# Storing results one pass later: a softmax-times-V kernel on one core

## The chip, the cores and the metric

The kernel runs on one core of a Trainium2 chip. A core has five engines that run side by side and signal each other with semaphores: TensorE (matmuls and transposes; PE in the profile, its weight loads PEld), VectorE (DVE), ScalarE (ACT), GpSimd (POOL) and SyncE (SP), which here does nothing but issue DMA transfers. The transfers themselves are carried out by 16 DMA engines. The metric is device time in microseconds (us), the median of several executions.

## The reference

```python
def reference(scores, v):               # scores 8 x 12 x 1024 x 1024, v 8 x 12 x 1024 x 64, float32
    scores_max = np.max(scores, axis=-1, keepdims=True)
    attn = np.exp(scores - scores_max)
    attn = attn / (np.sum(attn, axis=-1, keepdims=True) + 1e-8)
    return np.matmul(attn, v).astype(np.float32)
```

Batch and heads together are 96 independent heads (BH). The scores are 402.65 MB, V and the result 25.17 MB each, so a kernel that touches everything once moves 453 MB.

## The kernel before, in words

**Tiling.** Two heads are worked on together (T = 2): each has 64 of the 128 partitions, and each partition holds 16 consecutive rows of its head (R = 16). A "row" r below is therefore a tile of 128 partitions x 1024 scores, 512 KB in HBM. Two heads make a block of 16 rows (8 MB), two blocks (K = 2, k = 0 and 1) make a pass of four heads (AHEAD = 4), and the loop `with tc.For_i(0, BH, AHEAD)` runs 24 passes, n0 = 0, 4, ... 92.

**What happens to a row.** ScalarE takes the exponential and writes it as fp16 (L384; two rows per instruction, or one row where `late` holds). It subtracts no maximum. TensorE transposes the row in eight pieces into PSUM (L397), VectorE copies the transposed piece to SBUF (L409 for two rows, L405 for one row where `late` holds), and TensorE multiplies it in eight matmuls with V (L152, in `finish`). The V operand `vones` has a column of ones behind each head's 64 columns, so the product also holds the sum of the row. `finish` of a row comes LAG = 3 rows after its transposes. After every third row, and after row 15, VectorE takes the reciprocal of the sums (L132) and writes the quotient into `out_bufs[k]` (L140, `normalise`).

**Buffers.** There is one score buffer `s_bufs[k]` per block, 64 KB per partition, one result buffer `out_bufs[k]` per block, eight exp buffers of two rows (`p_bufs`), two of each for the transposed rows in PSUM and SBUF. A load into `s_bufs[k]` for the next pass can thus only be issued when ScalarE has read the last row of that block in this pass. `out_bufs[k]` may be written again only when its store has landed.

**V.** A DMA brings V of four heads into `v_sb` one pass ahead (`load_v`). GpSimd rearranges it into `vones[k]` with eight small casts (L255, `spread_v`): for k = 0 after row 15 of block 0, for k = 1 at the end of the pass.

**A guard.** Since no maximum is subtracted, the kernel watches its sums. ScalarE adds up the absolute values of `v_sb` (L266, `watch_v`), VectorE folds these and the reciprocals into a minimum and a maximum (`fold`, L284 and L285), and at the end `judge` counts the partitions in which all is in range. If any is not, a general routine is run instead; with this data it is not.

**The order of transfers.** SP issues all DMAs, in the order in which the code has them, and they go through one queue. In a pass the order is: next scores of block 0 (`load_first`, in the code at row 6 of block 1), store of block 0, next scores of block 1, store of block 1, V of two passes ahead (`last`). In all but the last passes a load is one DMA of 8 MB. In the passes n0 = 84 and 88 it is cut in pieces, (4, 6, 6) rows for block 0 and (4, 4, 4), then the store, then (2, 1, 1) for block 1. In pass 92 loads are skipped by a condition, and `end` stores block 1 in two parts, 12 rows and 4. The DMAs in the body take eight semaphores in turn, and a DMA waits until the one that last used its semaphore has landed.

**Order on the engines.** The order of TensorE's work is written out by `in_line`. The ifs on n0 are branches that each engine takes on its own; `branch_at` ties the branch of `load_first`, and that of `watch_v` (row 13 of block 1), to a place in TensorE's order.

Of the kernel before, what the change touches and what calls it, by code (L numbers as in the profile page):

```python
# [8 lines left out]
FP32 = mybir.dt.float32  # L9
FP16 = mybir.dt.float16  # L10
# [16 lines left out]
def kernel(  # L27
# [6 lines left out]
    nc = tc.nc  # L34
    P = 128
# [4 lines left out]
    BH = B * H  # L40
    assert SQ % P == 0 and SK % P == 0
    C = SK // P
    EB = 2
# [35 lines left out]
    def buffers(pool, count, shape, dtype, name):  # L79
        return [pool.tile(shape, dtype, name=f"{name}{k}") for k in range(count)]  # L80

    s_bufs = buffers(sb_pool, K, [P, R, SK], FP32, "s_nat")
    v_sb = sb_pool.tile([P, C // L, S, L, D], FP32, name="v_sb")
    p_bufs = buffers(sb_pool, 8, [P, EB, SK], FP16, "p_nat")
    pt_bufs = buffers(sb_pool, 2, [P, EB, SK], FP16, "pt")
    out_bufs = buffers(sb_pool, K, [P, R, D], FP32, "out_sb")
    small_pool = ctx.enter_context(tc.tile_pool(name="small", bufs=1))
    seen = small_pool.tile([P, 1 + K * R + 2], FP32, name="seen")
    nc.gpsimd.memset(seen, 1.0)
# [1 line left out]


    psO_bufs = buffers(ps_pool, 4, [P, 512], FP32, "psO")
    turn = {}

    def take(bufs):
# [8 lines left out]
    def after(a, b):  # L105

        tc.add_manual_dep(
            a.ins,
            b.ins.name,
            mybir.DependencyInfo(mybir.DependencyClass.NoSync, mybir.DependencyReason.DATA),  # L110
            reason="order",
        )
# [49 lines left out]
        if r == R - 1 and k < K - 1:  # L162
            spread_v(k)

    def store(n0, k):

        to = out_rows.rearrange("(m x) y -> m x y", x=P)[bass.ds((n0 + T * k) // T, 1)]
        to = to.rearrange("o x y -> (o x) y")
        send(nc.sync.dma_start(out=to, in_=out_bufs[k][:].rearrange("x r d -> x (r d)")))

    def send(dma):
        for other in stores:
            apart(dma, other)
            apart(other, dma)
        apart(dma, dma)
        stores.append(dma)
        queue(dma)

    def end():

        cut = (GROUPS - 2) * G
        for a, b in ((0, cut), (cut, R)):
            send(
                nc.sync.dma_start(
                    out=out_rows[(BH - T) * W : BH * W, a * D : b * D],
                    in_=out_bufs[K - 1][:, a:b].rearrange("x r d -> x (r d)"),
                )
            )

# [30 lines left out]
            )  # L220
            r += rows

    def branch_at(op):

        after(op, line[-1])

    def load_first(n0):

        before = queued[-1:]
        n = (n0 + AHEAD) % BH  # L230
        with tc.If(n0 < BH - 3 * AHEAD) as cmp:
            load(0, n)
            branch_at(queued[-1])
        with cmp.Else():
            queued[:] = before
            load(0, n, (4, 6, 6), cond=(n0 < BH - AHEAD))
            branch_at(queued[-1])
        line.append(queued[-1])

    def load_v(n, **cond):  # L240

# [20 lines left out]
    def watch_v():  # L262


        junk = p_bufs[0][:].rearrange("p r k -> p (r k)")
        return nc.scalar.activation(  # L266
            out=junk,
            in_=v_sb[:].rearrange("p h s l d -> p (h s l d)"),
            func=mybir.ActivationFunctionType.Abs,
            scale=1.0 / SUM_MAX,  # L270
            accum_out=seen[:, K * R + 1 : K * R + 2],
        )
# [78 lines left out]
    def last(n0, bank):  # L351

        before = queued[-1:]
        k = K - 1
        with tc.If(n0 < BH - AHEAD) as cmp:
            spread_v(k)
            n = (n0 + AHEAD + T * k) % BH
            with tc.If(n0 < BH - 3 * AHEAD) as cmp2:
                queued[:] = before
                load(k, n)  # L360
                store(n0, k)
                load_v((n0 + 2 * AHEAD) % BH)
            with cmp2.Else():
                queued[:] = before
                load(k, n, (4, 4, 4))
                store(n0, k)
                load(k, n, (2, 1, 1), 12)
                load_v(BH - AHEAD, cond=(n0 < BH - 2 * AHEAD))
        with cmp.Else():
            queued[:] = before  # L370
            end()
            judge(bank)

    def heads(n0):

        for k in range(K):
            st = dict(psO=[take(psO_bufs) for g in range(GROUPS)])
            for r in range(R):
                late = k == K - 1 and r >= R // 2
                if r % EB == 0:  # L380
                    p_nat, psT2, pt2 = take(p_bufs), take(psT_bufs), take(pt_bufs)
                    rows = 1 if late else EB
                    for g in range(0, EB, rows):
                        exp = nc.scalar.activation(  # L384
                            out=p_nat[:, g : g + rows, :].rearrange(
                                "p r (x v) -> p x r v", v=Q * L
                            ),
                            in_=s_bufs[k][:, r + g : r + g + rows, :].rearrange(
                                "p r (i x l) -> p x (r i) l", i=Q, l=L
                            ),  # L390
                            func=EXP,
                        )
                        rewrite(p_nat, exp)
                p_row = p_nat[:, r % EB, :].rearrange("p (h q l) -> p h l q", q=P, l=L)
                psT, pt = psT2[:, r % EB, :], pt2[:, r % EB, :]
                for c in range(C):
                    turned = nc.tensor.transpose(  # L397
                        out=psT[:, c * P : (c + 1) * P],
                        in_=p_row[:, c // L, c % L, :],
                        identity=ident16[:],  # L400
                    )
                    in_line(turned)
                    other_bank(psT2, r % EB, turned)
                if late:
                    copy = nc.vector.tensor_copy(out=pt, in_=psT)  # L405
                    rewrite(pt2, copy)
                    other_bank(psT2, r % EB, copy)
                elif r % EB == EB - 1:
                    copy = nc.vector.tensor_copy(out=pt2[:], in_=psT2[:])  # L409
                    rewrite(pt2, copy)  # L410
                if r == 6 and k == K - 1:
                    load_first(n0)
                    store(n0, 0)
                if r == 13 and k == K - 1:
                    with tc.If(n0 < BH - AHEAD):
                        watch = watch_v()
                        branch_at(watch)
                    line.append(watch)
                pending.append((n0, k, r, pt, st))
                while len(pending) > (LAG - 1 if late and r >= R - EB else LAG):  # L420
                    finish(pending.pop(0))
        while pending:
            finish(pending.pop(0))
        fold()
        last(n0, st["psO"][-1])
# [52 lines left out]
```

## Time and profile before

| what | value |
|---|---|
| runs | 1065.61, 1065.82, 1065.95 us; median 1065.82 |
| the profiled execution | 1065.58 us; its span, first to last instruction, 1063.8 us |
| DMA queue | 453 MB in 19584 packets, busy 99.1% of 16 engines' span, 426 GB/s on average |
| TensorE / weight loads | 77% / 74% of the span busy |
| ScalarE | 71%; 278.5 us of waiting for scores |
| VectorE / GpSimd | 66% / 22% |
| granted TensorE clock | 0.875 of full speed on average |
| one pass in the middle | about 43.6 us (load at 453.63, the same load of the next pass at 497.19) |

The page gives, for each engine, the time in which it was executing; a second part cuts the span in 40 slices and gives the busy share in tenths. A line such as "L384 ACT ..." is a group of instructions of one source line: busy time, mean duration in ns, then the idle time of the engine just before them and what ended it. In a timeline, a line is start, duration, engine, source line, operation, tiles, and in brackets the idle time ahead with its releaser. "Issue" lines of SP give the moment at which a DMA was put into the queue, not when it ran.

### The profile page before, as it was taken

How to read it: one execution, taken by the hardware profiler on the slowest of the kernel's cores; microseconds unless marked ns; L12 is line 12 of the kernel's file. 1: busy time of each engine (PE TensorE's matmuls, PEld its weight loads, DVE VectorE, ACT ScalarE, POOL GpSimd, SP SyncE). 2: the span in 40 equal slices, each digit the busy share in tenths (PEclk: the TensorE clock that was granted, in tenths of full speed). 3: DMA queues.
4: the chain of work that ended last, by engine and by line, in shares of the span. 5: the costliest groups of instructions: out<-in, count | busy, mean ns of one | idle time of the engine just before them, and what ended most of it. 6: DMA issues, size and time to landing. Idle time of an engine off the chain costs nothing. (4 is left out here: it accounts for less than half of the span.)

```text
span 1063.8 us, 33293 instructions
## 1 busy us (share of the span) xinstructions
PE 814.6 (77%) x12289; PEld 790.1 (74%) x12289; DVE 706.8 (66%) x1395; ACT 754.3 (71%) x530; POOL 239.0 (22%) x400
## 2 busy tenths in 40 slices
PE   2588778886877768886788778886788868887967
PEld 2488767786877768886777778876787867777967
DVE  1467766776667757676577765776667756677858
ACT  4477577776777667766777577775777667768965
POOL 3031130211312113112031130311312113112131
PEclk9788988888898978899888887998888898988989
DMA  9999999999999999999999999999999999999995
GB/s 394 435 429 431 414 434 453 414 453 430 418 453 414 432 455 414 453 414 432 452 416 451 407 443 451 416 448 427 426 448 419 423 437 441 414 453 413 430 415 228
DMA packets 19587, 453.04 MB, mean 426 GB/s; under 512 B 2176, under 2 KB 2304, under 8 KB 8960
## 3 DMA queue, kind: packets, MB, share of 16 engines
q1 hardware_dynamic: 19584, 452.99, 99.1%
q8 instruction: 3, 0.05, 0.0%
HBM read 437.26 MB, written 25.17 MB: 435 GB/s over the span
## 5 line engine op out<-in xcount | busy, mean ns | idle before, releaser
L384 ACT ACTIVATE p_nat<-s_nat 128x2048 f16<-128x2048 f32 (+1 forms) x480 | 707.1, 1557 | 292.5 <-DMA s_nat<-in_scores_dram 278.5
L397 PE MATMUL psT<-ident,p_nat 128*128 128x128 f16 x6144 | 525.5, 238 | 215.5 <-ACT p_nat L384 213.4
L397 PEld LDWEIGHTS <-p_nat 128*128 128x128 f16 x6144 | 442.3, 120 | 227.4 <-ACT p_nat L384 226.2
L409 DVE COPY pt<-psT 128x2048 f16<-128x2048 f16 x288 | 352.4, 1224 | 319.0 <-PE L152 159.0
L152 PE MATMUL psO<-vones,pt 128*128 128x130 f16 x6144 | 504.6, 229 | 28.4 <-DVE pt L405 17.7
L152 PEld LDWEIGHTS <-pt 128*128 128x128 f16 x6144 | 408.0, 102 | 40.7 <-DVE pt L405 21.9
L255 POOL CAST vones<-v_sb 32x512 f16<-32x512 f32 x392 | 238.1, 607 | 811.6 <-PE psT L397 360.9
L140 DVE TENSOR_TENSOR out_sb<-psO,seen 64x192 f32<-64x192 f32 (+1 forms) x576 | 192.0, 333 | 22.7 <-DMA out_dram<-out_sb 3.9
L405 DVE COPY pt<-psT 128x1024 f16<-128x1024 f16 x192 | 123.5, 684 | 2.3
L132 DVE RECIPROCAL seen<-psO 128x3 f32<-128x3 f32 (+1 forms) x288 | 49.6, 172 | 8.5 <-PE L397 4.7
L266 ACT ACTIVATE p_nat<-v_sb 128x2048 f16<-128x2048 f32 x24 | 45.6, 1900 | 1.0 <-DMA v_sb<-in_v_dram 1.0
L266 ACT ACT_TABLE_LOAD x1 | 1.3, 1283 | 5.8 <-DMA v_sb<-in_v_dram 5.8
L284 DVE TENSOR_REDUCE seen<-seen 128x1 f32<-128x34 f32 x24 | 4.5, 188 | 0.8
L266 ACT ACTIVATION_READ_ACCUMULATOR p_nat<-v_sb 128x1 f32 x24 | 4.5, 188 | 0.0
L285 DVE TENSOR_REDUCE seen<-seen 128x1 f32<-128x34 f32 x24 | 4.3, 178 | 0.0
L301 PEld LDWEIGHTS <-right 128*1 128x1 f16 x1 | 0.1, 79 | 1.8 <-DVE right L296 1.8
L301 PE MATMUL psO<-vones,right 128*1 128x1 f16 x1 | 0.2, 164 | 1.6 <-DVE right L296 1.6
L305 DVE CAST count<-psO 1x1 int32<-1x1 f32 x1 | 0.1, 147 | 0.3 <-PE psO L301 0.3
masks.py:199 POOL TENSOR_SCALAR_AFFINE_SELECT ident<-ident 128x128 f32<-128x128 f32 x1 | 0.3, 292 | 0.1
L74 ACT CAST ident<-ident 128x128 f16<-128x128 f32 x1 | 0.3, 282 | 0.0
masks.py:197 POOL MEMSET ident<- 128x128 f32 x1 | 0.2, 204 | 0.3 <-POOLq L462 0.3
L296 DVE SCALAR_TENSOR_TENSOR right<-seen,part 128x1 f16<-128x1 f32 x1 | 0.2, 161 | 0.0
(7 smaller groups left out, 0.8 us busy)
## 6 DMA issues: line engine op xcount, KB each, us to landing
v_sb<-in_v_dram SPq DMA_DIRECT2D x25, 1024.0 KB, 20.3
out_dram<-out_sb SPq DMA_DIRECT2D x47, 512.0 KB, 22.7
s_nat<-in_scores_dram SPq DMA_DIRECT2D x9, 2048.0 KB, 25.9
s_nat<-in_scores_dram SPq DMA_DIRECT2D x6, 3072.0 KB
s_nat<-in_scores_dram SPq DMA_DIRECT2D x2, 4096.0 KB, 18.7
s_nat<-in_scores_dram SPq DMA_DIRECT2D x2, 1024.0 KB
s_nat<-in_scores_dram SPq DMA_DIRECT2D x4, 512.0 KB
s_nat<-in_scores_dram SPq DMA_DIRECT2D x43, 28.4
```

What stands on the lines that cost most here:

```text
L132: nc.vector.reciprocal(out=recip, in_=psO[:, :, D : D + 1])
L140: nc.vector.tensor_tensor(out=out_bufs[k][part, g * G : g * G + rows, :], in0=psO[part, :, t * N : t * N + D], in1=recip[part].to_broadcas ...
L152: product = nc.tensor.matmul(out=st["psO"][g][:, i * M : (i + 1) * M], lhsT=pt[:, c * P : (c + 1) * P], rhs=vones[:, k, c].rearrange("p t ...
L255: nc.gpsimd.tensor_copy(out=vones[s * Q : (s + 1) * Q, k, :, t, 0:D].rearrange("i (h l) d -> i h l d", l=L), in_=v_sb[(k * T + t) * Q : (k ...
L266: return nc.scalar.activation(out=junk, in_=v_sb[:].rearrange("p h s l d -> p (h s l d)"), func=mybir.ActivationFunctionType.Abs, scale=1. ...
L284: nc.vector.tensor_reduce(out=seen[:, 0:1], in_=seen[:, 0 : n + 1], axis=X, op=ALU.min)
L285: nc.vector.tensor_reduce(out=seen[:, n + 1 : n + 2], in_=seen[:, 1 : n + 2], axis=X, op=ALU.max)
L301: nc.tensor.matmul(out=cell, lhsT=right[:], rhs=vones[:, 0, 0, 0, D : D + 1], start=True, stop=True)
L384: exp = nc.scalar.activation(out=p_nat[:, g : g + rows, :].rearrange("p r (x v) -> p x r v", v=Q * L), in_=s_bufs[k][:, r + g : r + g + ro ...
L397: turned = nc.tensor.transpose(out=psT[:, c * P : (c + 1) * P], in_=p_row[:, c // L, c % L, :], identity=ident16[:],)
L405: copy = nc.vector.tensor_copy(out=pt, in_=psT)
L409: copy = nc.vector.tensor_copy(out=pt2[:], in_=psT2[:])
```

## The change

Results no longer leave from `out_bufs` in the pass that made them. At the end of a pass GpSimd, behind its eight casts for block 1, copies both result buffers into two new buffers `done_bufs` (`put_by`). The stores of both blocks stand at the head of the next pass (`store_before`), ahead of all its loads in SP's order, and are skipped in pass 0. The last pass stores its own results in `end` straight from `out_bufs`: block 0 whole, block 1 in two parts. Loads no longer have stores between them. `load_first` stands at row 15 of block 0, without the ties to TensorE's order, and its pieces are (4, 4, 4, 4); block 1's pieces are (4, 4, 2, 2, 2, 2). The sum of absolute values stands behind row 15 of block 1 in every pass, the last one too, ahead of the fold, and writes its junk into the last exp buffer. There are six exp buffers instead of eight. Single-row exps and copies begin at row 12 of block 1 instead of row 8.

```diff
-    p_bufs = buffers(sb_pool, 8, [P, EB, SK], FP16, "p_nat")
+    p_bufs = buffers(sb_pool, 6, [P, EB, SK], FP16, "p_nat")
+    done_bufs = buffers(sb_pool, K, [P, R, D], FP32, "done")
...
+    for done in done_bufs:
+        nc.vector.memset(done, 0.0)
...
-    def store(n0, k):
-
-        to = out_rows.rearrange("(m x) y -> m x y", x=P)[bass.ds((n0 + T * k) // T, 1)]
-        to = to.rearrange("o x y -> (o x) y")
-        send(nc.sync.dma_start(out=to, in_=out_bufs[k][:].rearrange("x r d -> x (r d)")))
+    def put_by(k):
+
+        nc.gpsimd.tensor_copy(out=done_bufs[k][:], in_=out_bufs[k][:])
+
+    def store_before(n0):
+
+        for k in range(K):
+            n = (n0 + (BH - AHEAD + T * k)) % BH
+            to = out_rows.rearrange("(m x) y -> m x y", x=P)[bass.ds(n // T, 1)]
+            send(
+                nc.sync.dma_start(
+                    out=to.rearrange("o x y -> (o x) y"),
+                    in_=done_bufs[k][:].rearrange("x r d -> x (r d)"),
+                    cond=(n0 > 0),
+                )
+            )
...
         cut = (GROUPS - 2) * G
-        for a, b in ((0, cut), (cut, R)):
+        for k, a, b in ((0, 0, R), (1, 0, cut), (1, cut, R)):
+            n = BH - AHEAD + T * k
             send(
                 nc.sync.dma_start(
-                    out=out_rows[(BH - T) * W : BH * W, a * D : b * D],
-                    in_=out_bufs[K - 1][:, a:b].rearrange("x r d -> x (r d)"),
+                    out=out_rows[n * W : (n + T) * W, a * D : b * D],
+                    in_=out_bufs[k][:, a:b].rearrange("x r d -> x (r d)"),
                 )
             )
...
-    def branch_at(op):
-
-        after(op, line[-1])
-
     def load_first(n0):
 
         before = queued[-1:]
         n = (n0 + AHEAD) % BH
         with tc.If(n0 < BH - 3 * AHEAD) as cmp:
             load(0, n)
-            branch_at(queued[-1])
         with cmp.Else():
             queued[:] = before
-            load(0, n, (4, 6, 6), cond=(n0 < BH - AHEAD))
-            branch_at(queued[-1])
-        line.append(queued[-1])
+            load(0, n, (4, 4, 4, 4), cond=(n0 < BH - AHEAD))
...
-        junk = p_bufs[0][:].rearrange("p r k -> p (r k)")
-        return nc.scalar.activation(
+        junk = p_bufs[-1][:].rearrange("p r k -> p (r k)")
+        nc.scalar.activation(
...
             spread_v(k)
+            put_by(0)
+            put_by(1)
             n = (n0 + AHEAD + T * k) % BH
             with tc.If(n0 < BH - 3 * AHEAD) as cmp2:
                 queued[:] = before
                 load(k, n)
-                store(n0, k)
                 load_v((n0 + 2 * AHEAD) % BH)
             with cmp2.Else():
                 queued[:] = before
-                load(k, n, (4, 4, 4))
-                store(n0, k)
-                load(k, n, (2, 1, 1), 12)
+                load(k, n, (4, 4, 2, 2, 2, 2))
                 load_v(BH - AHEAD, cond=(n0 < BH - 2 * AHEAD))
...
     def heads(n0):
 
+        store_before(n0)
...
-                late = k == K - 1 and r >= R // 2
+                late = k == K - 1 and r >= R - 4
...
-                if r == 6 and k == K - 1:
+                if r == R - 1 and k < K - 1:
                     load_first(n0)
-                    store(n0, 0)
-                if r == 13 and k == K - 1:
-                    with tc.If(n0 < BH - AHEAD):
-                        watch = watch_v()
-                        branch_at(watch)
-                    line.append(watch)
+                if r == R - 1 and k == K - 1:
+                    watch_v()
```

## The prediction

> **What bounds the kernel now.** I read the page first: its slices and the queue's share.
>
> ```profile
> DMA  9999999999999999999999999999999999999995
> ...
> q1 hardware_dynamic: 19584, 452.99, 99.1%
> ...
> L384 ACT ACTIVATE p_nat<-s_nat 128x2048 f16<-128x2048 f32 (+1 forms) x480 | 707.1, 1557 | 292.5 <-DMA s_nat<-in_scores_dram 278.5
> L397 PE MATMUL psT<-ident,p_nat 128*128 128x128 f16 x6144 | 525.5, 238 | 215.5 <-ACT p_nat L384 213.4
> ```
>
> The transfers never stop until the last slice; ScalarE waits for scores, TensorE for ScalarE. So bytes through one queue set the time, and only two things can move the end: what lies in the queue ahead of the last scores, and what comes behind them. I then read busy shares by stretch (the last two columns are DMA share and GB/s).
>
> ```profile
> 453.00:497.00 44.00, 34.36 (x543) 33.20 (x541) 30.89 (x62) 31.79 (x24) 9.72 (x16) 0.92 0.99 429
> 1005.00:1048.50 43.50, 34.11 (x535) 33.02 (x532) 30.17 (x62) 30.03 (x21) 12.10 (x20) 0.92 1.00 420
> 1048.50:1052.00 3.50, 3.46 (x62) 3.31 (x60) 3.37 (x7) 3.50 (x5) 2.48 (x5) 1.00 0.21 85
> 1052.00:1063.80 11.80, 5.77 (x97) 5.33 (x94) 7.62 (x24) 1.58 (x2) 0.00 (x0) 0.85 0.22 89
> ```
>
> Full until 1048.5; then a fifth: a few of the 16 DMA engines trail by some 3 us. From 1052 on it is all tail. Next, one pass of SP's issues, for the lead of each transfer.
>
> ```profile
> 448.25 0.36 SPq L169 DMA_DIRECT2D out_dram<-out_sb  x1
> 453.63 0.35 SPq L217 DMA_DIRECT2D s_nat<-in_scores_dram  x1
> 461.14 0.36 SPq L169 DMA_DIRECT2D out_dram<-out_sb  x1
> 465.91 0.33 SPq L244 DMA_DIRECT2D v_sb<-in_v_dram  x1
> 476.36 0.34 SPq L217 DMA_DIRECT2D s_nat<-in_scores_dram  x1
> ```
>
> The load at 453.63 lands at 482.05, the store behind it at 483.35, V at 485.80. So the load at 476.36 is issued 9.4 us before the queue gets to it. Last, the last pass (n0 = 92) and the end; the first line is of the chain of waits, the others of the timeline.
>
> ```profile
> 1009.21 22.03 DMA out_dram<-out_sb
> 1030.05 5.51 ACT L384 ACTIVATE p_nat<-s_nat 128x2048 f16<-128x2048 f32 x3 [3.18 <-PE psT L397]
> 1031.34 0.74 DVE L140 TENSOR_TENSOR out_sb<-psO,seen 64x192 f32<-64x192 f32 x2 [3.90 <-DMA out_dram<-out_sb]
> 1033.39 0.67 PEld L152 LDWEIGHTS <-pt 128*128 128x128 f16 x7 [3.72 <-DVE pt L409]
> ...
> 1050.90 0.07 SPq L217 DMA_DIRECT2D s_nat<-in_scores_dram  x1
> 1052.10 0.07 SPq L217 DMA_DIRECT2D s_nat<-in_scores_dram  x1
> ...
> 1055.44 0.61 PE L397 MATMUL psT<-ident,p_nat 128*128 128x128 f16 x8
> 1056.96 0.69 DVE L405 COPY pt<-psT 128x1024 f16<-128x1024 f16 x1
> 1058.76 0.47 DVE L140 TENSOR_TENSOR out_sb<-psO,seen 64x64 f32<-64x64 f32 x2
> 1059.27 0.34 SPq L184 DMA_DIRECT2D out_dram<-out_sb  x1
> ```
>
> The store of pass 88's first result waits 22 us in the queue behind loads, VectorE's first normalise of pass 92 waits 3.90 us for it, and ScalarE (3.18) and TensorE (3.72) stop behind. From 1033.39 TensorE runs without a break, behind the data to the end. The two skipped loads stand there because each waits for the landing of the transfer that last used its semaphore: rows 14 and 15 of the scores landed at 1050.78 and 1051.98. Call that last landing T. From T to the last normalise takes 7.26 us (1059.24), to the last store's landing 9.14 (1061.12), to the span's end 11.8.
>
> **The change, part by part.** The sum starts from the profiled execution: 1065.58 us, 1.8 around a span of 1063.8. The median of the runs, 1065.82, is 0.24 above it, and I add that at the end.
>
> *Stores one pass later.* Ahead of T lie now 46 stores of 512 KB (passes 0 to 88). Afterwards 44: pass 88's two go out in pass 92, which SP issues behind the last load pieces. One costs the queue 1.28 us (a load landed at 1029.96, the store behind it at 1031.24). Two: T moves by -2.56, to 1049.4. In all other passes the bytes and their sizes are the same and the queue stays full: 0.
>
> *Where the covers are.* In a middle pass the order becomes load 0, load 1, V, two stores. The next load 0 then is issued as now, when ScalarE is done (14.7 us after its data landed), while the queue still holds the rest of load 1 (load to load 19.3 us), V 2.45 and stores 2.56: a lead of 9.6 us against 9.4. New on SP: the stores at the head of the pass wait for the second GpSimd copy, and load 0 is queued behind them. GpSimd spreads V until 465.67; then two copies of 128x1024. The nearest row, 32x512 in 607 ns, gives 1.2 us each by columns (taken: columns alone vary between it and the others), 4.9 if partitions counted too; the select of 128x128 in 292 ns gives 2.3. So the stores can go at 468.1 (bounds 468 to 475.5), before load 0 is ready at 476.4 and long before the queue has drained V near 485. Cost 0; a gain isn't possible in a full queue. VectorE's first normalise now waits for the first copy: 466.9 (to 470.6) against 470.36 in the trace: 0 to 0.3 us, under the same lead.
>
> *Smaller parts.* The sum of absolute values already runs behind all exps of a middle pass (453.42 behind them); there it stays, 2.1 us in ScalarE's 11 us of waiting. Six exp buffers instead of eight: ScalarE runs at 1.81 us a pair and TensorE's two rows at 1.82, so four buffers of lead hold both: 0. Fewer single-row exps save a few tenths under cover. The memsets on VectorE run while the first scores load (until 14.9 us). The skipped stores of pass 0 cost SP about 0.6 us each before 18 us, with loads queued until 44: 0.
>
> *Load pieces of the last two loads.* First block 4,4,4,4 for 4,6,6; second 4,4,2,2,2,2 for 4,4,4,2,1,1. By landings a row (512 KB) costs 1.21 in pieces of six, 1.22 in pieces of four, 1.23 in twos, 1.20 to 1.22 in ones: 0, bounds -0.3 to +0.3.
>
> The Trainium skill, "DMA: Bandwidth & Descriptors", section "Anatomy of one DMA", fits a transfer at about 2.0 us plus bytes over 436 GB/s, and its "Bandwidth" section asks for 1 MiB or more. If each piece paid that in the queue, the two additional pieces would cost an estimated 4 us and the sum would be 1065.1; the single rows, 1.20 to 1.22 us apart, show that queued pieces don't pay it.
>
> *Eight DMA semaphores taken in turn.* With two stores, up to four pieces, up to six and V, SP in pass 88 holds its stores for pieces 3 and 4 of the second load, and the first piece for pass 92 until piece 5 has landed. Then piece 6, V and two stores (7.5 us) still stand in the queue, 4 to 5 on the engines that are ahead; a DMA starts about 1 us after its issue. Taken 0; if it waited one transfer longer, up to +1.
>
> *The last pass.* No store is waited for: the first normalise needs the first GpSimd copy of pass 88. At worst TensorE ends pass 88 as now (1015.9), GpSimd spreads 5.3 us and copies 1.2 to 4.9: 1022.4 to 1026.3, against 1031.34. TensorE wins 1.20 - 0.91 = 0.3 us on the data with each row, so from there it has caught up long before T. The tail is then bare: two rows land at T; exps 0.95 + 1.04 with the start, T + 2.05; transposes 0.7 (T + 2.75); copy 0.69 (T + 3.45); then as now from that copy's end (1057.65) to the last normalise (1059.24) 1.59: T + 5.05. ScalarE's additional 2.1 us for the sum of absolute values end at T + 4.15, ahead of the fold: 0 (cover 0.9). The last store lands 1.85 after issue: T + 6.95, against 9.14: -2.19. Pass 88's stores occupy the queue until T + 2.6, the first block's store (SP gets to it at T + 2.3, past four skipped loads) until about T + 4.6, the next until 5.6; the last one's data starts at 6.1: 0, at worst +0.7.
>
> Sum: 1065.58 - 2.56 - 2.19 = 1060.8; with the 0.24, and nothing for the rest, **1061.1**.
>
> **Rivals.**
> *The tail takes its part back.* Something holds the last pass as the store does now: the copy on GpSimd, TensorE at half clock (8 transposes 1.04 instead of 0.61 us), or stores queued ahead of the last one. Only -2.56 remains: 1063.2. For it: the granted clock fell to 0.5 after each gap of over 3 us. Against it: stretches with TensorE 75% busy kept 1.0, and here rows of 0.91 come every 1.2 us.
> *Hidden anyway, or pieces that cost.* The last load's early end is eaten by a fixed price per piece, 2 us on two more pieces: 1065. The equal spacing of pieces speaks against it.
> *Slower: load 0 behind the stores on SP.* If the second copy ends so late that V has drained (485 less 1 us to start), the queue empties in each of 22 passes. That needs 8 us a copy instead of 1.2, beyond my upper bound of 4.9; each us more costs 22 us, so a copy of 8.5 us gives 1061 + 22 = 1083.
> *More.* The trailing of a few engines came from packets of up to 4.3 instead of 2.42 us at 62 to 66 us. If it stayed out, T would be up to 3.4 us earlier: 1057.7.
>
> **How the numbers follow.** Forecast (both gains whole, 1060.3 to 1062.0) 0.68; tail takes its part back, 1062.0 to 1063.7, 0.14; hidden 0.06; slower by the SP queue or another wait 0.06; more 0.06. From the forecast to the tail rival is 0.82, a little on each side for the bounds (+0.3, -0.3 on pieces, and half a lag below): 1059.6 to 1063.5. No change is within 0.2%, 2.1 us, about what a measurement of this kernel can tell; so faster 0.85 (forecast, more, nearly all of the tail rival), same 0.08, slower 0.07.
>
> **What would show it.** Right: DMA share 1.0 until about 1046 and the last score row landing near 1049.4; no VectorE wait for a store; waits of VectorE for GpSimd small; TensorE waiting for ScalarE in the last 10 us; the last exp ending 2 us after the last landing; stores of 512 KB running after it. Wrong: a DMA share under 0.97 in any middle stretch, SP's load issued after 480 in the pass shown, GpSimd copies over 5 us, TensorE still continuous behind the data at the end, or a last landing that hasn't moved.

## The result, and the profile after

The changed kernel takes 1068.92 us (median of eight runs, 1067.72 to 1069.74); the kernel before took 1065.66 us beside it. The ratio is 1.0032, 95% interval 1.0021 to 1.0043: slower by 0.3%, where the forecast was 1061.1. The profiled execution took 1067.72 us around a span of 1065.9.

First the page of the kernel after: its slices, its queue, and two groups of instructions.

```profile
DMA  9999999999999999999999999999999999999994
...
q1 hardware_dynamic: 19872, 452.99, 98.8%
...
L143 DVE TENSOR_TENSOR out_sb<-psO,seen 64x192 f32<-64x192 f32 (+1 forms) x576 | 191.8, 333 | 206.5 <-DMA s_nat<-in_scores_dram 187.1
...
L170 POOL COPY done<-out_sb 128x1024 f32<-128x1024 f32 x46 | 46.6, 1040 | 2.8
```

The queue is as full as before and GpSimd's copies are cheap (1.04 us). New is the third line: VectorE's normalise, which reads PSUM and writes the result buffer, waits 187.1 us for a load of scores into `s_nat`. It neither reads nor writes `s_nat`. The waits of VectorE give the number of times and the longest.

```profile
DVE out_sb L143 <- DMA s_nat<-in_scores_dram: 187.1, 22, 10.3
```

It happens in 22 of the 24 passes. In the middle it costs nothing: the load issued at 453.24 is issued again 43.9 us later, at 497.18, against 43.6 before, and the queue moves 429 GB/s in that stretch in both kernels. The busy shares by stretch (TensorE clock, DMA share and GB/s last) show where the time came from.

```profile
453.00:497.00 44.00, 33.12 (x517) 32.05 (x515) 29.17 (x57) 31.64 (x21) 11.78 (x19) 0.88 0.99 429
1005.00:1048.50 43.50, 35.72 (x584) 34.64 (x585) 33.04 (x66) 35.30 (x24) 13.75 (x22) 0.96 1.00 425
1048.50:1052.00 3.50, 3.41 (x61) 3.25 (x59) 3.33 (x6) 2.95 (x3) 2.85 (x5) 1.00 0.45 184
1052.00:1065.90 13.90, 7.91 (x129) 7.31 (x129) 9.47 (x25) 0.49 (x2) 0.00 (x0) 0.87 0.10 39
```

The scores are in earlier. The last score row lands at 1047.84 (T), 4.14 us before the 1051.98 of the kernel before. The tail from T to the last store's landing grew from 9.14 to 15.38 us (1063.22), that is by 6.24. The two together are +2.10, and the profiled executions differ by 2.14. One middle pass and the last pass, in the timeline of the kernel after (start, duration, engine, line, tiles, and in brackets the idle time ahead with its releaser), show what happens.

```profile
393.48 0.74 DVE L143 TENSOR_TENSOR out_sb<-psO,seen 64x192 f32<-64x192 f32 x2 [8.99 <-DMA s_nat<-in_scores_dram]
...
1028.20 0.17 DVE L135 RECIPROCAL seen<-psO 128x3 f32<-128x3 f32 x1
1029.95 0.61 PE L405 MATMUL psT<-ident,p_nat 128*128 128x128 f16 x8
1033.30 0.74 DVE L143 TENSOR_TENSOR out_sb<-psO,seen 64x192 f32<-64x192 f32 x2 [4.93 <-DMA s_nat<-in_scores_dram]
1035.36 1.04 PE L155 MATMUL psO<-vones,pt 128*128 128x130 f16 x8 [4.80 <-DVE pt L417]
1036.20 1.06 PE L405 MATMUL psT<-ident,p_nat 128*128 128x128 f16 x8
1037.05 1.07 PE L155 MATMUL psO<-vones,pt 128*128 128x130 f16 x8
1037.92 0.78 PE L405 MATMUL psT<-ident,p_nat 128*128 128x128 f16 x8
...
1059.08 0.69 DVE L413 COPY pt<-psT 128x1024 f16<-128x1024 f16 x1
1060.87 0.48 DVE L143 TENSOR_TENSOR out_sb<-psO,seen 64x64 f32<-64x64 f32 x2
```

In the last pass the reciprocal of block 0's first three rows is done at 1028.4; the quotient behind it starts at 1033.30. Just ahead of that, at 1033.18, the first piece (four rows) of block 1 has landed. VectorE holds its other work in order behind the waiting quotient, so TensorE stops for 4.80 us for want of a copied row, and starts again at half speed: three groups of eight matmuls take 1.04 to 1.07 us each and a fourth 0.78, instead of 0.61 to 0.63. From there it works to the end behind the data.

The experiments decide between these explanations.

**Theory A: a shared semaphore.** `end()` stores block 0 straight from `out_bufs[0]`. In the passes before the last no DMA touches that buffer any more, since GpSimd copies it away. But the loop's next normalise must be kept behind whatever may have read the buffer, and one branch of the loop body holds a DMA that reads it. In the turn of eight DMA semaphores that store has the one which, in the branch that runs in all other passes, belongs to block 1's load (its first piece where it is cut). In the trace one semaphore counts both, the landing of that piece at 1033.18 and that of the last pass's store of block 0 at 1052.29. So the wait "until the store has landed" becomes, in every pass, "until block 1's load has landed". This dependence is called the tie below. **Theory B:** the wait is put down to the load by the profile, but what really ends last is GpSimd's copy or something else the change added; then taking away the tie changes little. The texts of the expectations add a **theory C**: the stores that now lie behind the last scores hold up the last store.

### The profile page after: what moved, and what is told of

It is laid out like the page before. It is cut to its first block, busy times and chain, and to the rows that moved or that the text cites. A ratio compares the mean times of both kernels' runs of the same rounds, so it can differ in the third digit from the quotient of the medians.

```text
span 1065.9 us, 32432 instructions
## 1 busy us (share of the span) xinstructions
PE 781.5 (73%) x12289; PEld 755.5 (71%) x12289; DVE 701.7 (66%) x1349; ACT 761.4 (71%) x484; POOL 285.7 (27%) x446
## 5 line engine op out<-in xcount | busy, mean ns | idle before, releaser
L155 PEld LDWEIGHTS <-pt 128*128 128x128 f16 x6144 | 402.6, 102 | 241.0 <-DVE pt L417 209.9
L405 PE MATMUL psT<-ident,p_nat 128*128 128x128 f16 x6144 | 487.0, 228 | 59.8 <-ACT p_nat L392 34.0
L417 DVE COPY pt<-psT 128x2048 f16<-128x2048 f16 x336 | 409.4, 1223 | 145.6 <-PE L155 50.9
L405 PEld LDWEIGHTS <-p_nat 128*128 128x128 f16 x6144 | 412.1, 117 | 63.9 <-ACT p_nat L392 49.1
L143 DVE TENSOR_TENSOR out_sb<-psO,seen 64x192 f32<-64x192 f32 (+1 forms) x576 | 191.8, 333 | 206.5 <-DMA s_nat<-in_scores_dram 187.1
L274 ACT ACTIVATE p_nat<-v_sb 128x2048 f16<-128x2048 f32 x25 | 47.9, 1915 | 47.8 <-issue 45.0
L413 DVE COPY pt<-psT 128x1024 f16<-128x1024 f16 x96 | 63.4, 681 | 1.5
L170 POOL COPY done<-out_sb 128x1024 f32<-128x1024 f32 x46 | 46.6, 1040 | 2.8
```

Source lines behind the costliest of these rows:

```text
L143: nc.vector.tensor_tensor(out=out_bufs[k][part, g * G : g * G + rows, :], in0=psO[part, :, t * N : t * N + D], in1=recip[part].to_broadcas ...
L155: product = nc.tensor.matmul(out=st["psO"][g][:, i * M : (i + 1) * M], lhsT=pt[:, c * P : (c + 1) * P], rhs=vones[:, k, c].rearrange("p t ...
L170: nc.gpsimd.tensor_copy(out=done_bufs[k][:], in_=out_bufs[k][:])
L274: nc.scalar.activation(out=junk, in_=v_sb[:].rearrange("p h s l d -> p (h s l d)"), func=mybir.ActivationFunctionType.Abs, scale=1.0 / SUM ...
L405: turned = nc.tensor.transpose(out=psT[:, c * P : (c + 1) * P], in_=p_row[:, c // L, c % L, :], identity=ident16[:],)
```

## The experiments

**Without the tie.** No pass follows the one in which `end()` stores, so the dependence can be declared away. The changed kernel, otherwise whole:

```diff
-            nc.vector.tensor_tensor(
+            quotient = nc.vector.tensor_tensor(
...
+            quotients.append(quotient)
...
             send(dma)
+            for quotient in quotients:
+                apart(quotient, dma, "no pass follows the one that stores here")
```

> The changed kernel, but a normalise of the next pass no longer waits for the stores of the last pass's end (no pass follows those, so nothing else orders them). Theory A (shared semaphore): the first store in the end uses the semaphore that the load of block 1 uses in every other pass, so VectorE's first normalise of block 0 waits for that load (8.99 us in a middle pass, 4.93 us in the last); in the middle this is hidden under the transfers, in the last pass TensorE then runs without a break to the end. Without it: no VectorE wait for scores, the last score row still lands near 1047.8, the last store's landing 7 us behind it, 1059.3 us in all (1058.5 to 1061.5). Theory B (the other parts: six exp buffers, GpSimd copies, the sum of absolute values in the last pass): within 1 us of the changed kernel, 1068 to 1070. Theory C (the stores behind the last scores hold the last store up): half the way, 1062 to 1064, with TensorE caught up and the last store landing late after its issue.

Measured 1061.28 us (1061.16 to 1061.54), ratio to before 0.9957 (0.9943 to 0.9971); 7.6 us less than the changed kernel. (The kernel before took 1065.64 us beside this run and 1065.66 beside the changed kernel.) That is in the range of theory A alone. The waits of VectorE hold no load any more; the longest sum is for TensorE:

```profile
DVE pt L419 <- PE L407: 140.3, 22, 18.0
DVE pt L419 <- PE L156: 117.1, 87, 14.1
DVE pt L419 <- PE psO L156: 47.8, 56, 4.4
```

T is 1047.83, as in the changed kernel, and the last store lands at 1056.53, T + 8.70. The profiled executions of the two differ by 6.56 us, their tails by 6.68: 4.80 us of standing and about 1.4 us of half speed (from the restart the next four groups start 0.84, 0.85, 0.87 and 0.62 us apart, 3.18 in all, instead of 0.455 each) make 6.2 of that.

**The same by other data.** Here nothing is declared. In the last pass GpSimd copies block 0 away too, and `end()` stores it from `done_bufs[0]`, so that no DMA reads `out_bufs[0]` at all.

```diff
-                    in_=out_bufs[k][:, a:b].rearrange("x r d -> x (r d)"),
+                    in_=(done_bufs if k == 0 else out_bufs)[k][:, a:b].rearrange("x r d -> x (r d)"),
...
         with cmp.Else():
             queued[:] = before
+            put_by(0)
             end()
```

> The changed kernel, but the last pass too copies block 0 away on GpSimd and stores it from the copy, so that out_sb of block 0 is never read by a DMA: the wait goes by another buffer and no dependency is declared away. Theory A: as without the tie, 1059.3 us (1058.5 to 1061.5). Theory B: as the changed kernel, 1068 to 1070. Theory C: 1062 to 1064.

Measured 1061.45 us (1061.05 to 1061.54), ratio 0.9958 (0.9944 to 0.9971). T is 1047.86 and the last store lands at 1056.55. VectorE's wait for a load is gone here too, so it was not an effect of declaring something. Its normalise now waits for a GpSimd copy once, for 0.4 us:

```profile
DVE out_sb L143 <- POOL done L170: 0.4, 1, 0.4
```

**The tie put into the kernel before.** If the branch makes the wait, the old kernel must get it when the last pass stores block 0 in `end()`:

```diff
-        for a, b in ((0, cut), (cut, R)):
+        for k, a, b in ((0, 0, R), (1, 0, cut), (1, cut, R)):
+            n = BH - AHEAD + T * k
...
-                    store(n0, 0)
+                    store(n0, 0, cond=(n0 < BH - AHEAD))
```

> The kernel before, with one thing added: the last pass's store of block 0 stands in the end, as in the changed kernel, and the store at row 6 is skipped in that pass. Theory A: the end's first store again takes the semaphore of block 1's load; the first normalise of pass 92 waits for the first piece of that load (landing at 1036.1 in the profile of before) instead of the store (1031.3): 4.9 us more, 1070.5 (1069.5 to 1071.5), and waits of VectorE for scores in every pass. Theories B and C: no change, 1065.7 (1065 to 1066.5).

Measured 1070.78 us (1070.1 to 1071.26), ratio 1.0047 (1.0033 to 1.0061). The first line below is of VectorE's waits, the second of the timeline in the last pass.

```profile
DVE out_sb L140 <- DMA s_nat<-in_scores_dram: 194.8, 22, 11.6
...
1036.04 0.74 DVE L140 TENSOR_TENSOR out_sb<-psO,seen 64x192 f32<-64x192 f32 x2 [5.48 <-DMA s_nat<-in_scores_dram]
```

The same false wait, in as many passes, without any other part of the change. Again one semaphore counts both: block 1's first piece at 1035.92 and the last pass's store of block 0 at 1055.78.

**Moving the landing that is waited for.** If block 1's first piece ends the wait, its size sets the time. In the changed kernel the pieces (4, 4, 2, 2, 2, 2) of block 1 become, in two runs (the comments are not in the kernels):

```diff
-                load(k, n, (4, 4, 2, 2, 2, 2))
+                load(k, n, (2, 2, 4, 4, 2, 2))      # short first piece
+                load(k, n, (8, 2, 2, 2, 1, 1))      # long first piece
```

> The changed kernel with one size changed: the pieces of block 1's last loads are 2, 2, 4, 4, 2, 2 rows instead of 4, 4, 2, 2, 2, 2. Theory A: the piece that VectorE waits for lands two rows earlier (2.4 us), TensorE starts again 2.4 us earlier and all ends 2.4 us earlier: 1066.5 (1065.8 to 1067.3). Theories B and C: no change, 1068 to 1070.

> The changed kernel with one size changed: the pieces of block 1's last loads are 8, 2, 2, 2, 1, 1 rows instead of 4, 4, 2, 2, 2, 2. Theory A (VectorE's first normalise of the last pass waits for the first piece through the shared semaphore): the piece lands four rows later (4.85 us), so does TensorE's new start and the end: 1073.8 (1072.8 to 1075). Without that theory: no change, 1068 to 1070.

Measured 1064.46 us (1064.26 to 1065.69) and 1073.27 us (1073.11 to 1074.23), ratios 0.9989 (0.998 to 0.9998) and 1.0077 (1.0061 to 1.0092). The first pieces landed at 1031.00 and 1038.08. In the timelines of the last pass, the short piece first and then the long one:

```profile
1031.12 0.74 DVE L143 TENSOR_TENSOR out_sb<-psO,seen 64x192 f32<-64x192 f32 x2 [2.12 <-DMA s_nat<-in_scores_dram]
1033.18 0.64 PE L155 MATMUL psO<-vones,pt 128*128 128x130 f16 x8 [1.99 <-DVE pt L417]
```

```profile
1038.20 0.74 DVE L143 TENSOR_TENSOR out_sb<-psO,seen 64x192 f32<-64x192 f32 x2 [9.88 <-DMA s_nat<-in_scores_dram]
1040.26 1.05 PE L155 MATMUL psO<-vones,pt 128*128 128x130 f16 x8 [9.76 <-DVE pt L417]
```

The end of the wait follows the first piece: 1031.12, 1033.30 and 1038.20 for two, four and eight rows, while T stays within 0.3 us (1048.07, 1047.84, 1047.93). The long piece came out in its range. The short one came out 2.0 us under its number: the end of the wait moved by 2.2 us, near the 2.4 taken, but the stop of 1.99 us also left TensorE at full speed (0.64 us per eight), and that the forecast of this run had not counted. The two, 2.2 and about 1.4 us, account for the 3.5 us by which the tail shrank (15.38 to 11.90).

**Pieces and single rows.** The version without the tie, with the pieces and the single-row stretch of the kernel before:

```diff
-            load(0, n, (4, 4, 4, 4), cond=(n0 < BH - AHEAD))
+            load(0, n, (4, 6, 6), cond=(n0 < BH - AHEAD))
...
-                load(k, n, (4, 4, 2, 2, 2, 2))
+                load(k, n, (4, 4, 4, 2, 1, 1))
...
-                late = k == K - 1 and r >= R - 4
+                late = k == K - 1 and r >= R // 2
```

> The changed kernel without the tie, with the pieces of before (4, 6, 6 and 4, 4, 4, 2, 1, 1) and single-row exps and copies from row 8 on. If pieces and single rows cost nothing, as the prediction had it, the one-row last piece alone counts: one exp less behind the last landing, 1060.3 to 1061.3. If pieces or single rows cost: over 1062.

Measured 1061.35 us (1060.91 to 1061.89), ratio 0.9963 (0.9949 to 0.9976): no difference to 1061.28. T is 1048.33 and the tail 8.63.

**A last row by itself.** The tail was 8.70 where 6.95 had been worked out. Is it ScalarE's two exps behind T? The last piece cut into one and one:

```diff
-                load(k, n, (4, 4, 2, 2, 2, 2))
+                load(k, n, (4, 4, 2, 2, 2, 1, 1))
```

> The changed kernel without the tie, with the last piece of two rows cut in two pieces of one. If ScalarE's two exps behind the last landing set the tail, one of them (0.95 us) moves ahead of it: 1060.3. If VectorE and TensorE, which were busy without a break from 1048.6 on in the kernel without the tie, set it: no change, 1061.3.

Measured 1063.34 us (1062.89 to 1063.84), ratio 0.9981 (0.9972 to 0.999). The span of the profiled execution is 1059.5, no better than 1059.2; the loss lies outside the span: 3.4 to 4.0 us in all eleven runs, instead of 1.7 to 2.0. In this run's last 25 us, the DMA view lists two queues of instruction fetches, of which the version without the tie lacks the second:

```profile
q8 instruction: 1, 0.02, 0.2%
q14 instruction: 1, 0.01, 0.1%
```

It is a fetch of 8192 bytes at 1060.93, behind the last instruction of the span. To tell the row from the longer program, the same cut with block 0 in one piece less:

```diff
-            load(0, n, (4, 4, 4, 4), cond=(n0 < BH - AHEAD))
+            load(0, n, (4, 6, 6), cond=(n0 < BH - AHEAD))
...
-                load(k, n, (4, 4, 2, 2, 2, 2))
+                load(k, n, (4, 4, 2, 2, 2, 1, 1))
```

> The run that cut the last two rows into one and one gave 1063.34 us, with a span like that of the run without the cut and 1.5 us more outside the span, where one more fetch of instructions stood. Here the same last rows, but block 0 in 4, 6, 6, so that the number of pieces is ten again and the program is no longer. If the fetch made the loss: 1061.2 (1060.8 to 1061.6), with 1.8 to 2.0 us outside the span. If a last piece of one row costs by itself: 1063.3.

Measured 1061.67 us (1060.85 to 1062.31), ratio 0.9968 (0.9956 to 0.998), 1.8 us outside the span, and the further fetch is gone. T is 1048.13 and the tail 8.69. So the row by itself brings nothing. The loss and the further fetch came with the eleventh piece and went with it; that the fetch is what takes the time was not tested apart from that.

**Smaller bursts.** Perhaps the tail is long since four rows land at once:

```diff
-            load(0, n, (4, 4, 4, 4), cond=(n0 < BH - AHEAD))
+            load(0, n, (4, 6, 6), cond=(n0 < BH - AHEAD))
...
-                load(k, n, (4, 4, 2, 2, 2, 2))
+                load(k, n, (4, 2, 2, 2, 2, 2, 2))
```

> The changed kernel without the tie of VectorE's first normalise to the other block's load (as in the run that gave 1061.28 us), with the loads cut into 4, 6, 6 rows for block 0 and 4, 2, 2, 2, 2, 2, 2 for block 1: the same ten pieces in all. If the 8.70 us from the last score row's landing to the last store's landing are long because four rows land at once and are then worked off at some 0.6 us per two rows, VectorE is nearer to the data when the last row lands: the stretch is 7.3 to 7.5 us, the last row still lands at 1047.8, and the time is 1060.1 (1059.5 to 1060.8). If the backlog comes from VectorE's and TensorE's own pace and not from bursts, 1061.3.

Measured 1061.12 us (1060.82 to 1062.16), ratio 0.9964 (0.9951 to 0.9978): not to be told from 1061.28. T is 1048.00, the tail 8.61. In this run TensorE does not wait for ScalarE after 1023.19. Without the tie and with the old bursts it waits for it as late as 1040.08, for a row of a four-row piece that landed at 1038.03. Yet row 15's transposes start at much the same distance from T (1051.13, T + 3.13, against 1051.03, T + 3.20). But block 0's last piece was a burst of six here, so bursts as such are not cleared.

**Only the old wait away.** The prediction priced the old wait of VectorE for a store (3.90 us) at 2.19 us of tail. To try that alone, the kernel before with the store of block 0 moved behind the first piece of the load, once in the last three passes (n0 = 84, 88 and 92), once in the last two alone:

```diff
-                    store(n0, 0)
...
-            load(0, n, (4, 6, 6), cond=(n0 < BH - AHEAD))
+            load(0, n, (4,), cond=(n0 < BH - AHEAD))
+            store(n0, 0)          # or: cond n0 = 88 and 92 here, n0 = 84 behind the pieces
+            load(0, n, (6, 6), 4, cond=(n0 < BH - AHEAD))
```

> The kernel before with one transfer moved: in passes 84 and 88 the store of block 0 stands behind the first piece (4 rows) of the next load of block 0 instead of behind all three. No store leaves the queue ahead of the last scores, so T stays; only the 3.90 us wait of VectorE in the last pass goes. If that wait is what the tail carried, the tail shortens from 9.1 us to the 7 to 8.7 us that the kernels without a wait show: 1064.3 (1063.3 to 1065.0). If TensorE's own rate held the tail: no change, 1065.6.

> The kernel before with the store of block 0 put behind the first piece of load 0 in the last pass that loads and the pass before it alone, so that VectorE's last wait for a store (3.90 us in the profile before) goes and no data is moved behind the last scores. If the wait carried the 2.19 us that the prediction took for the tail: the stretch from the last row's landing to the end falls to 6.95 us and the time is 1063.5. If VectorE has rows to work off in any case: the stretch is 8.4 us as in the run with the early store in an earlier pass, and with the last row at 1052 the time is 1065.0 (1064.3 to 1065.5). If SP, held by that store until VectorE has normalised, issues the pieces behind it too late again, the queue runs dry before the last rows, and the time is over 1066.

Measured 1067.54 us (1066.84 to 1068.29), ratio 1.002 (1.0011 to 1.0029), and 1070.48 us (1069.86 to 1070.89), ratio 1.0047 (1.0033 to 1.0061). The first misses its forecast; the second meets the third of its cases, over 1066. The cause is the same. The lines are of SP's issues and of the busy shares by stretch, first of the one run, then of the other:

```profile
948.48 0.34 SPq L217 DMA_DIRECT2D s_nat<-in_scores_dram  x1
970.38 0.36 SPq L169 DMA_DIRECT2D out_dram<-out_sb  x1
971.35 3.50 SPq L217 DMA_DIRECT2D s_nat<-in_scores_dram  x4
```

```profile
965.00:975.00 10.00, 10.00 (x161) 9.85 (x159) 8.05 (x17) 10.00 (x10) 4.85 (x8) 0.91 0.65 242
```

```profile
971.17 0.11 SPq L169 DMA_DIRECT2D out_dram<-out_sb  x1
...
965.00:975.00 10.00, 10.00 (x147) 9.90 (x145) 7.42 (x14) 10.00 (x10) 4.85 (x8) 0.82 0.49 185
```

SP waits at the store until VectorE has normalised block 0, the pieces behind it come 22.9 us after the first, and the queue runs dry (DMA share 0.65; in the kernel before 1.01 in the same stretch). In the second run the store of that pass is skipped by its condition, and SP waited for VectorE all the same, 22.6 us until 971.17; the share was 0.49. T moved to 1054.02 and 1055.79. What the runs tell of the wait itself: in both VectorE's wait for a store is 1.1 us instead of 3.90, and the tails are 8.45 and 8.35 instead of 9.14. So an estimate for the old wait is 0.7 to 0.8 us of tail, not 2.19, with two reserves: 1.1 us of it was left, and the late data also gave the engines time to catch up.

**VectorE's queue in the tail.** Without the tie VectorE works from 1046.09 to its last normalise with one break of 0.19 us. The copies of the last two rows go to ScalarE, first as they are ordered by themselves, then with ScalarE's sum of absolute values put behind them (the comments are not in the kernels):

```diff
-                    copy = nc.vector.tensor_copy(out=pt, in_=psT)
+                    if r >= R - 2:
+                        copy = nc.scalar.copy(out=pt, in_=psT)
+                        moved.append(copy)                 # second run alone
+                    else:
+                        copy = nc.vector.tensor_copy(out=pt, in_=psT)
...
-        nc.scalar.activation(
+        watch = nc.scalar.activation(
             out=junk,
...
+        for copy in moved:                                 # second run alone
+            after(watch, copy)
```

> The changed kernel without the tie (1061.28 us), and the copies of the last two rows' transposed scores out of PSUM (0.69 us each on VectorE) done by ScalarE, which has no exp left there. In the run without the tie VectorE worked without a break from 1046.09 to the last normalise at 1054.65, and the copies of these two rows ended at 1051.5 and 1053.07. If VectorE's queue sets the 8.70 us from the last score row's landing (1047.83) to the last store's landing, ScalarE copies row 14 at 1050.3 to 1051.3 and row 15 at 1051.7 to 1052.7 (its single-row exps take 1.0), the last normalise ends near 1054.0, the stretch falls to 8.0 us and the time to 1060.6 (1060.2 to 1061.0). If the order of TensorE's rows sets it, the stretch stays at 8.7 and the time at 1061.3; if ScalarE's copies, waiting for transposes, hold back the next exps in the middle passes, the period of a pass grows over 43.6 us and the time is over 1062.

> The kernel with the copies of the last two rows on ScalarE (1061.71 us), with ScalarE's sum of absolute values put behind these copies. There the sum stood ahead of both, from 1050.0 to 1052.0, the copies ran from 1051.90 to 1053.80, and VectorE waited 1.56 us for them. Now the copies can run at 1050.4 to 1051.4 and 1051.8 to 1052.8. If VectorE's queue set the stretch from the last score row's landing to the last store's landing in the run without the tie (8.70 us), the last normalise ends near 1054.0 instead of 1054.65, the stretch is 8.0 us and the time 1060.6 (1060.2 to 1061.0). The sum of absolute values then ends near 1054.9 and the fold and the count come after the last normalise by 0.3 us more: if the count sets the end of the span, the stretch is 8.0 but the time stays at 1061.3. If TensorE's order of rows sets the stretch, it stays at 8.7.

Measured 1061.71 us (1061.49 to 1061.95), ratio 0.9966 (0.9952 to 0.9979), and 1061.58 us (1060.86 to 1062.02), ratio 0.9962 (0.9949 to 0.9976). In the timeline of the first run ScalarE's sum (L276) came ahead of its copies, so they ended later than VectorE's had:

```profile
1050.00 1.90 ACT L276 ACTIVATE p_nat<-v_sb 128x2048 f16<-128x2048 f32 x1
1051.81 0.19 ACT L276 ACTIVATION_READ_ACCUMULATOR p_nat<-v_sb 128x1 f32 x1
1051.90 1.90 ACT L416 COPY pt<-psT 128x1024 f16<-128x1024 f16 x2
```

The second run answers the question. Row 15's path in the version without the tie (T = 1047.83), and then in the second run (T = 1048.40):

```profile
1051.03 0.61 PE L407 MATMUL psT<-ident,p_nat 128*128 128x128 f16 x8
1052.38 0.69 DVE L415 COPY pt<-psT 128x1024 f16<-128x1024 f16 x1
1054.17 0.48 DVE L143 TENSOR_TENSOR out_sb<-psO,seen 64x64 f32<-64x64 f32 x2
```

```profile
1051.60 0.61 PE L410 MATMUL psT<-ident,p_nat 128*128 128x128 f16 x8
1052.46 1.01 ACT L419 COPY pt<-psT 128x1024 f16<-128x1024 f16 x1 [0.43 <-PE psO L157]
1054.61 0.47 DVE L144 TENSOR_TENSOR out_sb<-psO,seen 64x64 f32<-64x64 f32 x2
```

The transposes of row 15 start at T + 3.20 in both. The copy starts 0.74 us behind the transposes on VectorE, 0.25 us behind them on ScalarE, but takes 1.01 instead of 0.69. The tail is 8.57 instead of 8.70. Taking the copies off VectorE brought 0.13 of the 0.7 us that the expectation named for the case that VectorE's queue sets the tail, and nothing in time. Most of the lateness is there when TensorE gets to row 15: of the 1.75 us by which the tail exceeds the predicted 6.95, 1.15 are the transposes' T + 3.20 instead of T + 2.05.

## Why the prediction was wrong, point by point

**The step that failed** is the first sentence of *The last pass*: "No store is waited for: the first normalise needs the first GpSimd copy of pass 88." In *Where the covers are* it stands as "VectorE's first normalise now waits for the first copy". Both followed the buffer through the branch that runs, and forgot the DMA in the branch that doesn't. The prediction knew that eight semaphores are taken in turn, and counted what SP waits for by them; it didn't ask what VectorE would wait for by the same turn. The price, from the run without the tie: 6.6 us in profiled executions, 7.6 in medians, and it turned a gain of 4.4 us (1065.64 to 1061.28) into a loss of 3.3. It is shown by two independent removals, by the old kernel with the tie, and by the end of the wait following the size of the first piece.

The rival *the tail takes its part back* named the right kind of event, something that holds the last pass as the store does now, with TensorE at half speed. It counted as its worst that the tail keeps its old length (1063.2). It grew by 6.24 us, since the new wait ended 2 us later than the old one (normalise at 1033.30 instead of 1031.34) while the data came 4 us earlier. The slower rival, load 0 behind the stores on SP, did not happen: GpSimd's copies took 1.04 us and the load was issued in time. The chances had 0.06 for "slower by the SP queue or another wait"; another wait it was, and no line of the prediction said which.

**The sum, by terms**, read in the version without the tie, where the failed step is out:
- *Two stores behind the last scores, T by -2.56*: T moved by -4.15, to 1047.83. The direction and the -2.56 stand as far as bytes go, the rest was not in the sum. In the kernel before, the queue had a slow spell between 1020 and 1030 us that the kernels with the change lack there; the busy shares show 389 GB/s in that stretch before, 434 in the version without the tie, though the DMA share is full in both. The landings of the last piece on the 16 DMA engines divide the -4.15: their mean moved by -3.17 (1049.48 to 1046.31), which fits the two stores and some 0.6 us of the spell; the other -0.98 is that the slowest engine trails this mean by 1.52 us instead of 2.51. This is the rival *more* in part.
- *Tail by -2.19, to 6.95*: the tail is 8.70, so -0.44. "TensorE wins 1.20 - 0.91 = 0.3 us on the data with each row, so from there it has caught up long before T" was too good: row 15's transposes start at T + 3.20, where T + 2.05 was taken; its copy ends at T + 5.24 instead of T + 3.45. TensorE had caught up, since it still waits for ScalarE at 1040.08, but that wait is for the four rows landed at 1038.03, and from there it needs 10.95 us for eleven rows. In the last 14 us TensorE and VectorE have little to spare: VectorE copies two rows in 1.23 us and spends 0.95 us on each three rows' quotient, about 0.93 us a row, and the last four rows are copied one by one at 0.66 to 0.69.
- So -4.15 and -0.44, together -4.59, come near the predicted -4.75, by errors of opposite sign. That the version without the tie lands on 1061.28 is luck, and no proof of the working.
- *Load pieces, single rows: 0* was right (1061.35 with the old ones). So was it to charge no piece the fixed 2.0 us or so of the Trainium skill, "DMA: Bandwidth & Descriptors", section "Anatomy of one DMA", whose fit is for transfers issued by GpSimd: no run shows such a cost per piece in this queue, which SP keeps full.
- *Middle passes: 0* was right, even with a false wait of up to 10.3 us in 22 passes: a full queue hides it. *GpSimd copies of 1.2 us* measured 1.04. *The sum of absolute values ahead of the fold: 0*: in the version without the tie it ends at 1051.82, the fold starts at 1054.68.

One of the signs named as proof of an error did appear: TensorE still continuous behind the data at the end.

## What to carry to other kernels

When a loop body has branches, look at every DMA that touches a buffer, the ones in branches that hardly ever run included, and ask which semaphore the loop will wait on for it and which transfer counts up that semaphore in the branch that does run. A wait for a transfer that the instruction has nothing to do with is the sign; the cure is to let no DMA in the rare branch read the loop's buffer, or to declare what can't follow. And a tail is not bare because its engines are faster than the data on average: read at the last landing how many rows they are behind.

## What the runs showed of the hardware

- **Half speed after a stop.** TensorE came back at full speed after standing 1.99 us (0.64 us per eight matmuls), and at half speed after 4.80 and 9.76 us (1.04 to 1.07 for three and for five groups). The Trainium skill, "TensorE: Matmul & The Clock Gate", Part 1, puts the edge at an idle window of about 3.4 us; the three stops here agree with that. The edge is not sharp in these runs: in the kernel before a stop of 3.19 us (until 1023.32) led to half speed too, and in the run with small bursts one of 2.67 us did so 1.1 us after the restart (granted clock 0.50 from 1024.8 on).
- **One semaphore for two things costs time.** The Trainium skill, "DMA: Bandwidth & Descriptors", section "Why a DMA increments its semaphore by 16 and not by 1", wants one semaphore per in-flight slot; its reason is that a wait on a shared one can pass too early. Here the sharing made a wait pass too late, for 187 us in all and 4.93 us where it counted.
- **A skipped DMA still waits.** In the kernel before with the early store, SP stood 22.6 us, until 971.17, for a store that its condition then skipped, and the queue ran dry behind it (DMA share 0.49).
- **Code fetches behind the end.** With one more load piece came a fetch of 8192 bytes behind the last instruction, and 3.4 to 4.0 us outside the span instead of 1.7 to 2.0; the second run with the early store had such a fetch too, at 1069.37, with 4.0 to 4.2 us outside its span. That the fetch is the cause is likely, but not shown.
- **Slow spells.** For a few microseconds early in the run most packets of the queue take longer, about 1 us per engine on average: at 62 to 67 us in the kernel before (packets of up to 4.30 instead of 2.42 us), at 84 to 90 us in the changed kernel and the version without the tie. Afterwards some engines trail the others by 2.3 to 2.9 us, depending on the kernel, for as long as the queue is full. The kernel before has the second spell at 1020 to 1030 us and trails by 3.4 us behind it. What causes the spells stays open; no experiment bears on it. Where the queue ran dry, the trailing shrank to 0.6 us.
